# Taking a kernel's short first load from its large group instead of from one contiguous megabyte, with three stores in place of four

## The chip, the cores and the metric

The kernel runs on one core of one Trainium2 chip. The metric is the time of one execution on the device, in microseconds (us). The trace records every DMA packet.

## The reference

```python
batch, channels, length = 32, 256, 4096          # x: 134 MB of fp32
output_size = 256
for i in range(output_size):
    start = int(i * length / output_size)
    end = int((i + 1) * length / output_size)
    result[:, :, i] = np.max(x[:, :, start:end], axis=-1)
```

Each output is the maximum of 16 neighbouring inputs. Nothing is reused: 134.22 MB are read and 8.39 MB are written.

## The kernel before

One window is 16 floats, 64 bytes. There are 16,384 windows for each of 128 partitions. They are fetched in 20 loads, all issued by SyncE, into three slots of one large tile. VectorE reduces each load, and the results collect at the top of the same tile. Loads are at first 1,024 windows (64 KB) per partition and shrink as the results take room. The first load is short, 128 windows (8 KB), so that VectorE has something to do early.

```python
    slot_sizes = [MOST]                              # MOST = 1024 windows
    rounds = [[FIRST] + [MOST] * (SLOTS - 1)]        # FIRST = 128, SLOTS = 3
    # ... later rounds shrink: 1000, 940, 884, 832, 784, 736+152 ...
    sizes = [n for r in rounds for n in r]
    groups = [sizes[:1], sizes[1 : ROUNDS_A * SLOTS], sizes[ROUNDS_A * SLOTS :]]
    # ...
    for g, loads in enumerate(groups):
        n = sum(loads)
        xg = xw[first : first + P * n].rearrange("(p n) w -> p (n w)", p=P)
        og = ow[first : first + P * n].rearrange("(p n) -> p n", p=P)
        # ...
        for i, size in enumerate(loads):
            a = b - size
            # ...
            nc.sync.dma_start(out=slot, in_=xg[:, a * W : b * W])
            nc.vector.reduce_max(out=area[:, base + a : base + b], in_=..., axis=X)
        # ...
        if g < len(groups) - 1:
            stores.append((og, area[:, base : base + n]))
        else:                                        # LAST = 4: the last four loads apart
            end = sum(loads[len(loads) - LAST :])
            for a, b in ((end, n), (0, end)):
                stores.append((og[:, a:b], area[:, base + a : base + b]))
    for dst, src in stores[1:2] + stores[0:1] + stores[2:]:
        nc.sync.dma_start(out=dst, in_=src)
```

A group is a contiguous part of x that is dealt out to the partitions. So a group of n windows per partition has a distance of 64 n bytes between the rows of two neighbouring partitions: its partition pitch. The first group is 128 windows: one contiguous megabyte, in 128 rows of 8 KB. The second is 7,868 windows (pitch 491.75 KB, KB being 1,024 bytes), the third 8,388 windows (524.25 KB).

## Time and profile before

| | before |
|---|---|
| time, median of 3 | 335.2 us (335.18 to 335.23) |
| moved over the span | 142.61 MB, 428 GB/s |
| DMA queue busy | 99.2% of the span |
| VectorE busy | 83% |

From the page of the kernel before: the span, VectorE's busy time and share, DMA packets, the DMA queue's share of 16 engines' span, and the costliest group of instructions with VectorE's idle time and what ended it.

```profile
span 333.4 us, 113 instructions
DVE 276.0 (83%) x20; POOL 0.2 (0%) x4
DMA packets 3456, 142.61 MB, mean 428 GB/s; under 512 B 384, under 2 KB 512, under 8 KB 512
q1 hardware_dynamic: 3456, 142.61, 99.2%
L82 DVE TENSOR_REDUCE area<-area 128x1000 f32<-128x16000 f32 (+8 forms) x20 | 276.0, 13806 | 49.2 <-DMA area<-in_x_dram 49.2
```

The queue's 99.2% is what counts. VectorE is busy 83% and waits for loads in the rest; the DMA engines hardly wait for anything. The Trainium skill, "DMA: Bandwidth & Descriptors", section "Bandwidth", gives 425 GB/s as measured for one large load into all partitions (16 MB, issued there from GpSimd, here from SyncE), and 435 as the ceiling. The trace agrees: the second and third load, 8.39 MB each, end 19.35 us apart, which is 434 GB/s.

The start in the timeline of the kernel before (start, duration, engine and instruction, then the idle time ahead of it and what ended it):

```profile
5.60 2.29 DVE L82 TENSOR_REDUCE area<-area 128x128 f32<-128x2048 f32 x1 [5.60 <-DMA area<-in_x_dram]
24.95 17.22 DVE L82 TENSOR_REDUCE area<-area 128x1024 f32<-128x16384 f32 x1 [17.06 <-DMA area<-in_x_dram]
44.30 17.22 DVE L82 TENSOR_REDUCE area<-area 128x1024 f32<-128x16384 f32 x1 [2.13 <-DMA area<-in_x_dram]
63.20 16.82 DVE L82 TENSOR_REDUCE area<-area 128x1000 f32<-128x16000 f32 x1 [1.68 <-DMA area<-in_x_dram]
```

The stores among its DMA issues (transfer, engine and operation, count, KB of one, us from issue to landing):

```profile
out_dram<-area SPq DMA_DIRECT2D x1, 3934.0 KB, 27.4
out_dram<-area SPq DMA_DIRECT2D x1, 2966.0 KB, 33.7
out_dram<-area SPq DMA_DIRECT2D x1, 1228.0 KB, 7.3
out_dram<-area SPq DMA_DIRECT2D x1, 64.0 KB, 27.1
```

Their 27 and 34 us are queueing: the first three are issued at about 295 us, behind loads that last until 312 us. The last waits for the last reduce and is issued at 325.2 us, while the engines are still busy until 329 us with the store before it. So nothing at the end is exposed except the 1.3 us between the last completion write (332.07 us) and the end of the span.

### The profile page before, as it was taken

The page shows a single profiled execution, that of the slowest core. Times are in us where ns is not written, and L with a number is a line of the kernel's source. Part 1 is how long each engine was busy: PE and PEld are TensorE (multiplying, and loading weights), DVE is VectorE, ACT ScalarE, POOL GpSimd, SP SyncE. Part 2 cuts the span into 40 slices and gives each one's busy share as a digit, 9 for nine tenths or more (in the row PEclk, how much of TensorE's full clock was granted, in tenths as well). Part 3 has the DMA queues.
Part 4 walks back from the last instruction along what each step waited for, and adds up shares of the span by engine and source line. Part 5 has one row for each costly group of instructions (what it writes and reads, how often), then busy time and mean ns, then how long its engine had stood idle before and what let it go on. Part 6 is the DMA issues. An engine that isn't in the chain of part 4 may idle for free.

```text
span 333.4 us, 113 instructions
## 1 busy us (share of the span) xinstructions
DVE 276.0 (83%) x20; POOL 0.2 (0%) x4
## 2 busy tenths in 40 slices
DVE  2009979797988989797989797989898898989990
POOL 0000000000000000000000000000000000000000
DMA  9898989898989998999999999999999999999997
GB/s 377 377 503 377 503 369 491 369 491 369 491 369 462 462 462 346 462 462 441 434 434 434 434 434 415 409 409 505 415 409 433 433 433 433 433 416 452 391 432 333
DMA packets 3456, 142.61 MB, mean 428 GB/s; under 512 B 384, under 2 KB 512, under 8 KB 512
## 3 DMA queue, kind: packets, MB, share of 16 engines
q1 hardware_dynamic: 3456, 142.61, 99.2%
HBM read 134.22 MB, written 8.39 MB: 428 GB/s over the span
## 4 chain that ended last, share of the span: by engine, by line
DMA 64%; DVE 31%; DVEq 1%; another core or an unknown queue 0%; SPq 0%; issue 0%
DMA area<-in_x_dram 64%; DVE area L82 31%; DVEq L129 1%; SPq L81 0%; DVEq L82 0%
## 5 line engine op out<-in xcount | busy, mean ns | idle before, releaser
L82 DVE TENSOR_REDUCE area<-area 128x1000 f32<-128x16000 f32 (+8 forms) x20 | 276.0, 13806 | 49.2 <-DMA area<-in_x_dram 49.2
L115 POOL MEMSET const-bfloat16-1.0<- 128x1 bf16 x1 | 0.1, 102 | 0.0
L115 POOL MEMSET const-uint8-127<- 128x1 uint8 x1 | 0.1, 102 | 0.0
L115 POOL MEMSET const-float32-0.0<- 128x1 f32 x1 | 0.1, 99 | 0.2 <-issue 0.2
L115 POOL MEMSET const-float32-1.0<- 128x1 f32 x1 | 0.1, 99 | 0.0
## 6 DMA issues: line engine op xcount, KB each, us to landing
area<-in_x_dram SPq DMA_DIRECT2D x3, 8000.0 KB, 39.9
area<-in_x_dram SPq DMA_DIRECT2D x3, 7520.0 KB, 37.5
area<-in_x_dram SPq DMA_DIRECT2D x3, 7072.0 KB, 35.3
area<-in_x_dram SPq DMA_DIRECT2D x3, 6656.0 KB, 33.2
area<-in_x_dram SPq DMA_DIRECT2D x3, 6272.0 KB, 31.3
area<-in_x_dram SPq DMA_DIRECT2D x1, 5888.0 KB, 30.3
out_dram<-area SPq DMA_DIRECT2D x1, 3934.0 KB, 27.4
out_dram<-area SPq DMA_DIRECT2D x1, 2966.0 KB, 33.7
```

Of the source, the lines that this page charges most:

```text
L82: nc.vector.reduce_max(out=area[:, base + a : base + b], in_=slot.rearrange("p (n w) -> p n w", w=W), axis=mybir.AxisListType.X,)
L115: nc = _bacc.Bacc("TRN2", target_bir_lowering=False, num_devices=1)
L129: with _tile.TileContext(nc) as tc:
```

## The change

The intent: one group fewer, so one store fewer. The store that falls away is the short one, with rows of 512 bytes. In exchange the first load's rows come from the large group, which grows to 7,996 windows (pitch 499.75 KB); they no longer form one contiguous megabyte.

```diff
-    groups = [sizes[:1], sizes[1 : ROUNDS_A * SLOTS], sizes[ROUNDS_A * SLOTS :]]
+    groups = [sizes[: ROUNDS_A * SLOTS], sizes[ROUNDS_A * SLOTS :]]
...
-    for dst, src in stores[1:2] + stores[0:1] + stores[2:]:
+    for dst, src in stores:
         nc.sync.dma_start(out=dst, in_=src)
```

Sizes and order of the loads, VectorE's instructions and the addresses in the tile stay the same.

## The prediction

> **What bounds the kernel now.** The page gives 428 GB/s and a DMA queue 99.2% busy; VectorE is busy 276.0 of 333.4 us, and its 49.2 us of idle time are waits for loads. The packet records show data moving without a gap from 1.75 us to the last completion write at 332.07 us: loads until about 312.4, the 31,472-byte rows of the large store until 321.8, the 512-byte rows of the small store (0.195 us of each engine), the 23,728-byte rows until 329.1, the last 9,824-byte rows. So the span is the sum of the transfers on each of 16 engines, with 1.75 us before and 1.3 us after. Only transfer time, start-up latency or a new hole changes it. The last store is issued at 325.2 us, 3.4 us before its engines come free.
>
> **What the change does, costed.**
> 1. It removes the small store: eight 512-byte packets per engine (24 ns apart) and a completion write of under 10 ns, 0.20 us of each engine. The bytes return as 512 more in each of eight 31 KB rows, at 26.9 GB/s: 8 x 19 ns = 0.15 us. Net gain 0.05 us.
> 2. The first large group's pitch becomes 499.75 KB instead of 491.75. The Trainium skill, "DMA: Bandwidth & Descriptors", "Latency and other measured facts", reports [...]full rate at a padded large pitch. This trace has the mirror case: the second group's pitch is 524.25 KB, 12.25 KB above 512 where the new one is 12.25 below; the two sum to 1 MB. Its rows run at 27.0 GB/s per engine, spread under 1% (50,176 bytes in 1.853 to 1.864 us), like the first group's. I expect no aliasing and no change for loads 2 to 9.
> 3. The first load reads 8 KB rows 499.75 KB apart instead of one contiguous megabyte. Now: first packets take 0.3 to 1.3 us (median near 0.95), all later ones 0.309, which is full rate; VectorE starts at 5.60 us. The second load already begins at scattered rows directly behind 8 KB packets, and its first 64 KB packets take 2.418 us, full rate too: a scattered row's first access is hidden behind one 8 KB packet. So only the very first packets can be longer, by 0 to 0.5 us, my estimate from their present spread. All of it is critical: nothing later has a hole to absorb it.
> 4. VectorE's instructions, SBUF addresses and the order of loads stay; the first slot is released near 7.9 us, some 35 us before its next load is needed.
>
> **Sum.** -0.05 us (store) + 0.15 us (start) = +0.1: 335.3 us, range 334.9 to 336.3. Chances: faster by over 2% 1%, within 2% 97%, slower by over 2% 2%.
>
> **What would show it.** Right: first reduce at 5.5 to 6.2 us; later reduces shifted by the same amount; later 8 KB packets at 0.309 us; 64,000-byte rows at 2.36 us; no 512-byte packets; last store's rows directly after the second's. Wrong at 2 if packets of loads 2 to 9 take longer; wrong at 3 if later 8 KB packets exceed 0.309 us or the landing moves by over 0.7 us.
>
> **What would make it wrong.** Address conflicts at the new pitch (tens of us if they halve the rate of half the loads); a start-up stall on every scattered 8 KB packet (8 x 0.5 = 4 us at most).

## The result

| | before | changed |
|---|---|---|
| median of 6 runs, same chip | 335.19 us (335.16 to 335.23) | 335.09 us (334.88 to 335.18) |
| ratio | | 0.9996, 95% interval 0.9983 to 1.0009 |

Ratios are the mean time of one kernel's fast runs over that of the other's in the same rounds, so not quite the ratio of the medians.

The changed kernel's page:

```profile
span 333.4 us, 112 instructions
DVE 276.0 (83%) x20; POOL 0.2 (0%) x4
DMA packets 3312, 142.61 MB, mean 428 GB/s; under 512 B 368, under 2 KB 368, under 8 KB 368
q1 hardware_dynamic: 3312, 142.61, 99.1%
L81 DVE TENSOR_REDUCE area<-area 128x1000 f32<-128x16000 f32 (+8 forms) x20 | 276.0, 13806 | 49.1 <-DMA area<-in_x_dram 49.1
```

There are 144 packets fewer: 128 rows of 512 bytes and 16 completion writes. There is one instruction fewer, and no busy time, rate or share on the page moves by more than 0.1. Its timeline at the start:

```profile
5.22 2.29 DVE L81 TENSOR_REDUCE area<-area 128x128 f32<-128x2048 f32 x1 [5.22 <-DMA area<-in_x_dram]
24.71 17.22 DVE L81 TENSOR_REDUCE area<-area 128x1024 f32<-128x16384 f32 x1 [17.20 <-DMA area<-in_x_dram]
44.26 17.22 DVE L81 TENSOR_REDUCE area<-area 128x1024 f32<-128x16384 f32 x1 [2.33 <-DMA area<-in_x_dram]
63.17 16.82 DVE L81 TENSOR_REDUCE area<-area 128x1000 f32<-128x16000 f32 x1 [1.69 <-DMA area<-in_x_dram]
```

And its stores among the DMA issues:

```profile
out_dram<-area SPq DMA_DIRECT2D x1, 3998.0 KB, 27.6
out_dram<-area SPq DMA_DIRECT2D x1, 2966.0 KB, 34.2
out_dram<-area SPq DMA_DIRECT2D x1, 1228.0 KB, 7.4
```

One line is odd. The first reduce begins 0.38 us earlier with the scattered rows, where the prediction had it 0.15 us later. By the third reduce only 0.04 us of that is left. The packet records show where it went: the first load's packets cost less, but some rows of loads 2 and 3 took up to 2.56 us instead of 2.42. The engines' ends, worked out from the completion writes of each load (mean of 16 engines, and the last one):

```
                     load 1           load 3            last load          end of all stores
before   mean/last   4.973 / 5.174    43.644 / 43.833   312.280 / 312.487  331.841 / 332.063
changed  mean/last   4.737 / 4.872    43.481 / 43.926   312.116 / 312.514  331.652 / 332.040
```

The mean engine keeps 0.16 us of the early start to the last load, but the last engine keeps none, and the kernel ends with the last one. Is the early start the change's doing, or did this one execution happen to have it? That is the first question for the experiments.

### The profile page after: what moved, and what is told of

It is laid out like the page before. It is cut to its first block, busy times and chain, and to the rows that moved or that the text cites. A ratio compares the mean times of both kernels' runs of the same rounds, so it can differ in the third digit from the quotient of the medians.

```text
span 333.4 us, 112 instructions
## 1 busy us (share of the span) xinstructions
DVE 276.0 (83%) x20; POOL 0.2 (0%) x4
## 3 DMA queue, kind: packets, MB, share of 16 engines
HBM read 134.22 MB, written 8.39 MB: 428 GB/s over the span
## 4 chain that ended last, share of the span: by engine, by line
DMA 64%; DVE 31%; DVEq 1%; another core or an unknown queue 0%; SPq 0%; issue 0%
DMA area<-in_x_dram 64%; DVE area L81 31%; DVEq L128 1%; SPq L80 0%; DVEq L81 0%
```

## The experiments

(A completion write is the 4-byte packet with which each engine ends each transfer; "the mean engine" is the mean of the 16 engines' times.) Theory A: the contiguous megabyte costs the start some tenths of a microsecond, and scattering its rows wins them. Rival B: the start varies from run to run, and only the store's price is the change's own. Each session below is a set of kernels run on one chip with the kernel before among them. Session 1 is the result above; session 2 ran on chip 9, session 3 (the later sections) on chip 4, sessions 4 and 5 on chip 12. Because the tail is far more regular than the start, the stores are compared by the time of the mean engine from its last load's completion to its final completion.

### Both kernels again, and each part of the change alone

The kernel before and the changed one, unaltered:

> The kernel before, once more, for a second profile. If the slow start is a property of the contiguous first megabyte, first 8 KB packets again take about 0.95 us in the median, the start costs about 0.7 us per engine over full rate, and the first reduce starts at 5.6 us. If the start differs by chance from run to run, these numbers will differ by 0.2 us or more from the first profile. Time 335.2 us.

> The changed kernel, once more. Theory (scattered first rows start faster): first reduce at about 5.2 us, start costs about 0.35 us per engine, one or two engines lose 0.2 to 0.4 us in loads 2 to 4 again. Rival (chance): these numbers wander, and the first reduce may be at 5.6 us or later. Time 335.1 us, ratio to before 0.9997.

The loads of the change with the small store put back:

```diff
-            stores.append((og, area[:, base : base + n]))
+            cut = n - FIRST
+            for a, b in ((0, cut), (cut, n)):
+                stores.append((og[:, a:b], area[:, base + a : base + b]))
```

> The changed kernel with its large store cut in two, so that the 512-byte rows and the fourth store are back while the loads stay scattered. If the store is worth 0.05 us: the mean engine's end moves back by 0.05 us (0.20 us for the small store against 0.15 us), time about 335.15 us. If the store were what made the change faster, the time returns to 335.2 us and the start stays at 5.2 us.

The stores of the change with the contiguous first load put back (the first 128 windows are wrong):

```diff
-            nc.sync.dma_start(out=slot, in_=xg[:, a * W : b * W])
+            src = xg[:, a * W : b * W]
+            if n_loads == 0:
+                src = xw[: P * size].rearrange("(p n) w -> p (n w)", p=P)
+            nc.sync.dma_start(out=slot, in_=src)
```

> The changed kernel with only the first load taken from the contiguous first megabyte of x (results of the first 128 windows wrong on purpose); pitch of the large group and the three stores as in the change. If contiguity costs the start: first reduce at 5.6 us, 0.7 us per engine, time about 335.15 us (only the store's 0.05 us is left). If chance: start as in the changed kernel, 5.2 us.

In later sessions, three more looks at the start. First, the changed kernel a third time:

> The changed kernel a third time, in a session of its own. If the 0.1 us of the first session (335.09 against 335.19 us) and its early start (first reduce at 5.22 us) were chance: 335.18 us, first reduce near 5.55 us, third load's mean landing near 43.62 us. If scattered rows can gain 0.1 us: a time of 335.1 us or less, and a third load's landing near 43.5 us.

Second, the kernel before with only its first load scattered:

```diff
-            nc.sync.dma_start(out=slot, in_=xg[:, a * W : b * W])
+            src = xg[:, a * W : b * W]
+            if n_loads == 0:
+                src = xw[P * size : P * (size + 7868)].rearrange("(p n) w -> p (n w)", p=P)[:, (7868 - size) * W : 7868 * W]
+            nc.sync.dma_start(out=slot, in_=src)
```

> The kernel before with only the first load's source changed: 8 KB rows 491.75 KB apart, from the large group (first 128 windows wrong on purpose); the small store stays. If scattering costs or saves the start anything, first reduce and third load's landing move against 5.5 to 5.6 and 43.61 to 43.65 us, as by the prediction's 0.15 us later; if not, they stay and the time is 335.2 us.

Third, the contiguous variant of the changed kernel once more:

> The changed kernel with the contiguous first load once more, in another session (first 128 windows wrong on purpose). So far the first reduce began at 5.53 to 5.60 us in three profiles with a contiguous first load, and at 5.22, 5.28, 5.54, 5.54, 5.58 and 5.63 us in six with a scattered one. If the early start is chance, it may show here too, at 5.2 to 5.3 us; if only scattered rows can have it, this is again 5.5 to 5.6 us. One look can show that a contiguous load has early starts, and cannot show that it has none. Last load to end, mean engine: 22.476 us again.

(The 22.476 us in this text counts from the end of the last load but one; the table below counts from the last load.) What was measured, with the two first profiles:

| session | run | first load | small store | first reduce, us | load 3, mean engine | last load to end, mean engine | time, median | the kernel before in that session |
|---|---|---|---|---|---|---|---|---|
| 1 | before | contiguous | yes | 5.60 | 43.644 | 19.562 | 335.19 | |
| 1 | changed | scattered | no | 5.22 | 43.481 | 19.536 | 335.09 | 335.19 |
| 2 | before_again | contiguous | yes | 5.53 | 43.607 | 19.563 | 335.16 | 335.19 |
| 2 | after_again | scattered | no | 5.54 | 43.607 | 19.540 | 335.18 | 335.19 |
| 2 | after_split_store | scattered | yes | 5.54 | 43.647 | 19.632 | 335.20 | 335.19 |
| 2 | after_first_contiguous | contiguous | no | 5.57 | 43.652 | 19.540 | 335.22 | 335.19 |
| 4 | after_third | scattered | no | 5.28 | 43.475 | 19.540 | 335.11 | 335.38 |
| 4 | before_first_scattered | scattered, 491.75 KB | yes | 5.63 | 43.563 | 19.562 | 335.21 | 335.38 |
| 5 | after_first_contiguous_2 | contiguous | no | 5.64 | 43.699 | 19.540 | 335.23 | 335.24 |

The first reduce in four of these looks: before_again, after_again, after_third and after_first_contiguous_2.

```profile
5.53 2.29 DVE L82 TENSOR_REDUCE area<-area 128x128 f32<-128x2048 f32 x1 [5.53 <-DMA area<-in_x_dram]
5.54 2.29 DVE L81 TENSOR_REDUCE area<-area 128x128 f32<-128x2048 f32 x1 [5.54 <-DMA area<-in_x_dram]
5.28 2.29 DVE L81 TENSOR_REDUCE area<-area 128x128 f32<-128x2048 f32 x1 [5.28 <-DMA area<-in_x_dram]
5.64 2.29 DVE L84 TENSOR_REDUCE area<-area 128x128 f32<-128x2048 f32 x1 [5.64 <-DMA area<-in_x_dram]
```

*The start.* The same changed kernel began its first reduce at 5.54 us in session 2, so the 0.38 us of the first profile is not something that scattered rows always win. Nor do they cost the predicted 0.15 us: 5.54 us lies within the contiguous looks, 5.53 to 5.64. Theory A in its plain form falls. The packets say so too: the time that an engine's eight 8 KB packets took over eight times 0.309 us was 0.69 us in the first profile of the kernel before, but 0.40 us in before_again, where 0.7 was expected, and lies at 0.27 to 0.69 us in the four contiguous looks and at 0.35 to 0.65 us in the six scattered ones. What remains is that early starts (5.22 and 5.28) came in two of five looks at the changed kernel's loads (after_8_small_stores, below, has 5.58), and in none of four with a contiguous first load. In after_third the expectation for a real gain was met (335.11 us, load 3 at 43.475 us). But the kernel before was slow in that session (335.38 us), and the other scattered start there, before_first_scattered, had 5.63 us and 335.21 us. With so few looks, chance is not ruled out, nor a difference between chips, and neither is an early start that only scattered rows can have. Even where it came, it did not reach the end in the profile: in after_third the mean engine's load 3 ended at 43.475 us, but its last load at 312.305, later than in the first profile of before (312.280), because rows of loads 2 to 12 ran slow here and there (60,160-byte rows took up to 2.453 us instead of 2.22). Slow rows are no mark of scattered first rows or of an early start: after_first_contiguous_2 had 64 KB rows of up to 2.634 us, with neither, in the slowest execution of its set (335.70 us). The two executions with an early start were also the slowest of their sets (335.18 and 335.45 us), so it stays open whether the faster ones, which have no trace, kept the early start.

*The stores.* Here the columns hardly scatter. In the kernel before, again, and with a scattered first load 19.562, 19.563 and 19.562 us pass; with the change's stores 19.536 and four times 19.540, whichever way the first load is read. So the change's store part is worth 0.02 us of the mean engine, not 0.05. To split this by store, each engine's packets have to be followed in the records, each beginning where the engine's last one ended. Sorting the completion writes by time does not do: the engines are some 0.4 us apart and the small store lasts only 0.2 us, so the writes of two stores mix. Engine by engine:

```
mean engine, us           large store (with the small one)   second store   last store
before                    9.335 + 0.195 = 9.530              7.060          2.972
before_again              9.336 + 0.195 = 9.531              7.061          2.972
changed                   9.482                              7.075          2.979
after_again               9.484                              7.077          2.979
after_split_store         9.334 + 0.194 = 9.528              7.126          2.977
```

The small store takes 0.195 us and its bytes in long rows 0.149 us (9.484 less 9.335), a difference of 0.046 us, as predicted. But the second store, which has the same rows in both kernels, is 0.017 us longer in the changed one (its 23,728-byte rows take 0.8871 and 0.8874 us in the mean instead of 0.8852), and the last 0.007 us longer. The first load has no part in it: after_first_contiguous has 9.484, 7.077 and 2.978. Why the same rows are slower was not found. Putting the small store back behind the longer pitch cost 0.09 us of the mean engine (19.632 against 19.540), not the expected 0.05: half of that is the small store again, and half is the second store, whose first rows took 0.940 us there, 0.892 in the changed kernel and 0.882 in the kernel before. So a small store ahead does not by itself make the rows behind it slower.

### Multiplying the price of a small store

The difference above is too small to see in a time, so the suspected cost was multiplied.

```diff
-            stores.append((og, area[:, base : base + n]))
+            cuts = [0] + [n - k * FIRST for k in range(8, -1, -1)]
+            for a, b in zip(cuts, cuts[1:]):
+                stores.append((og[:, a:b], area[:, base + a : base + b]))
```

> The changed kernel with its large store cut into one of 6,972 windows per partition and eight of 128 (512-byte rows). The prediction's price (0.20 us for a small store against 0.15 us for the same bytes in long rows) makes the mean engine's end 8 x 0.05 = 0.4 us later, all of it in the span: about 335.6 us. The price that the four profiles so far show, from the end of the last load to the end of the large store's bytes (9.551 against 9.483 us), makes it 8 x 0.07 = 0.55 us. If the end of the kernel hides it, 335.2 us.

Measured: 336.12 us (336.05 to 336.57) against 335.18 for the kernel before, ratio 1.003, interval 1.0017 to 1.0042. The price is in the span, as expected, but it is larger than either sum. The page and its DMA issues:

```profile
DMA packets 4464, 142.61 MB, mean 427 GB/s; under 512 B 496, under 2 KB 1520, under 8 KB 1520
out_dram<-area SPq DMA_DIRECT2D x1, 3486.0 KB, 26.4
out_dram<-area SPq DMA_DIRECT2D x1, 2966.0 KB, 8.7
out_dram<-area SPq DMA_DIRECT2D x8, 64.0 KB, 25.8
```

The mean engine needs 20.57 us from its last load to the end, 1.03 more than the changed kernel. By the row records 8.281 us of this are the large store, 7.106 the second and 2.988 the last (7.077 and 2.979 in the changed kernel), which leaves 2.196 us for the eight small stores: 0.275 us each, where a single one took 0.195. The bytes of one piece take 0.150 us in long rows ((9.484 - 8.281) / 8), so each piece costs 0.12 us and all eight 0.99; only 0.04 us lies in the stores behind them. The 512-byte packets themselves became longer along the row of small stores, from 0.027 us among the first 256 to 0.036 us later on; the mean is 0.033. Why was not found. The prediction, which priced one small store, came to less than half. (The 0.07 us in the expectation came from completion writes sorted by time, the mixing described above; followed engine by engine it is 0.05.)

### The pitch

The prediction quoted from the Trainium skill a halved rate at a row pitch of 512 KiB. That is a misreading. The page ("DMA: Bandwidth & Descriptors", section "Latency and other measured facts") has 207 GB/s at 512 KiB, beside 214 for full rate; the halved figure, 103, belongs to 4 and 8 MiB, and 2 MiB has 164, all for copies between HBM tensors. So four runs asked what an exact power of two does in this kernel. "The page" in their expectations is this one, and the times worked out there from its figures are estimates.

One group, a pitch of exactly 1 MB, two stores, results right:

```diff
-    groups = [sizes[: ROUNDS_A * SLOTS], sizes[ROUNDS_A * SLOTS :]]
+    groups = [sizes]
```

> The changed kernel with one group, so that every load has a partition pitch of exactly 1 MB; two stores; results right. If a pitch at a power of two aliases, by the halving that the prediction wrongly attributed to 512 KB, 65,536-byte rows would take about 5 us and the time is near 640 us; between the figures that the page really has for 512 KB (207 of 214 GB/s) and 2 MB (164), rows take 3 to 30% longer: 345 to 420 us. If the pitch does not matter here: rows at 2.42 us and 335.2 us.

The same with the loads' pitch 8 KB shorter (source rows overlap, results wrong):

```diff
-            nc.sync.dma_start(out=slot, in_=xg[:, a * W : b * W])
+            src = bass.AP(tensor=x.tensor, offset=a * W, ap=[[(n - 128) * W, P], [1, size * W]])
+            nc.sync.dma_start(out=slot, in_=src)
```

> The one-group kernel with the partition pitch made 8 KB less than 1 MB in the loads and nothing else changed (overlapping source rows, results wrong on purpose). If the 8.7 us of the one-group kernel were the exact power of two, rows return to 2.42 us and the time to 335.2 us, as the page says of 4 KB of padding. If they came of having one group, or of any pitch near a power of two, the time stays near 344 us.

Both groups at exactly 512 KB, by a longer first load, and a control with the same loads and other pitches:

```diff
-    FIRST = 128
+    FIRST = 348
-    ROUNDS_A = 3        # (control only)
+    ROUNDS_A = 4
```

> The changed kernel with a first load of 348 windows instead of 128, which makes both groups 8,192 windows: a pitch of exactly 512 KB in every load. By the page's figure at 512 KB (207 of 214 GB/s, 3%): rows of 64 KB at 2.5 us and a time near 345 us; if the pitch does not matter: 2.42 us, 335 to 336 us.

> Control of pitch_512: the same loads and instructions of VectorE, the groups cut one round later, so that the pitches are 677 and 347 KB. Rows at full rate, 2.42 us; 335 to 336 us. The difference of the two is the pitch's alone, but for the stores' row lengths.

| pitch of the loads | time, median | range | the kernel before in that session |
|---|---|---|---|
| 1 MB | 343.88 us | 342.77 to 345.80 | 335.18 |
| 1 MB less 8 KB | 335.21 us | 335.12 to 335.50 | 335.38 |
| 512 KB, both groups | 335.82 us | 335.57 to 336.81 | 335.18 |
| 677 and 347 KB (control) | 335.28 us | 335.27 to 335.35 | 335.18 |

An exact 1 MB costs 8.7 us (ratio 1.0248, interval 1.0226 to 1.0270), and 8 KB less restores it all, in one group and with two stores. An exact 512 KB costs about 0.5 us against its control: the 64 KB rows take 2.427 us instead of 2.420 in the mean, the 63,744-byte rows 2.372 instead of 2.354. That is under 1% in these rows, less than the 3% between the page's two figures. The two kernels' store rows differ in length as well.

The unexpected part is when the 1 MB kernel pays. Its timeline (loads 2 to 8; the traced execution was the slowest of its set, 345.80 us):

```profile
28.78 17.22 DVE L81 TENSOR_REDUCE area<-area 128x1024 f32<-128x16384 f32 x1 [20.53 <-DMA area<-in_x_dram]
50.27 17.22 DVE L81 TENSOR_REDUCE area<-area 128x1024 f32<-128x16384 f32 x1 [4.27 <-DMA area<-in_x_dram]
71.34 16.82 DVE L81 TENSOR_REDUCE area<-area 128x1000 f32<-128x16000 f32 x1 [3.85 <-DMA area<-in_x_dram]
90.69 16.82 DVE L81 TENSOR_REDUCE area<-area 128x1000 f32<-128x16000 f32 x1 [2.53 <-DMA area<-in_x_dram]
109.72 16.82 DVE L81 TENSOR_REDUCE area<-area 128x1000 f32<-128x16000 f32 x1 [2.21 <-DMA area<-in_x_dram]
129.06 15.82 DVE L81 TENSOR_REDUCE area<-area 128x940 f32<-128x15040 f32 x1 [2.52 <-DMA area<-in_x_dram]
146.79 15.82 DVE L81 TENSOR_REDUCE area<-area 128x940 f32<-128x15040 f32 x1 [1.92 <-DMA area<-in_x_dram]
```

The eighth load's reduce in the kernel before:

```profile
136.55 15.82 DVE L82 TENSOR_REDUCE area<-area 128x940 f32<-128x15040 f32 x1 [1.89 <-DMA area<-in_x_dram]
```

What moved in four stretches of that kernel (from and to, length, VectorE and GpSimd busy with counts, TensorE's clock, mean DMA share, GB/s):

```profile
6.00:44.00 38.00, 17.47 (x2) 0.00 (x0) 1.00 0.99 381
44.00:63.00 19.00, 14.73 (x2) 0.00 (x0) 1.00 1.00 389
63.00:82.00 19.00, 15.14 (x2) 0.00 (x0) 1.00 0.97 408
82.00:101.00 19.00, 16.47 (x2) 0.00 (x0) 1.00 1.02 441
```

And in the same stretches of the kernel with 8 KB less:

```profile
6.00:44.00 38.00, 19.19 (x2) 0.00 (x0) 1.00 1.01 439
44.00:63.00 19.00, 17.22 (x1) 0.00 (x0) 1.00 1.01 435
63.00:82.00 19.00, 16.82 (x1) 0.00 (x0) 1.00 1.00 431
82.00:101.00 19.00, 16.82 (x1) 0.00 (x0) 1.00 0.99 428
```

The rate is 381 GB/s at first and rises; VectorE's idle time ahead of the eighth load's reduce, 1.92 us, is again that of the kernel before (1.89), and the mean engine takes 17.74 us for load 9, against 17.75 in the changed kernel. From there the loads but the very last run at full rate. Meanwhile the engines drift apart: their completions of one load spread over 0.6 us at load 1, 2.3 at load 3 and 3.9 at load 9, where the same kernel with 8 KB less stays under 0.9 us throughout. That fits engines that collide while they walk their rows in step and stop colliding once they are out of step; no run tests that reading. The spread is paid once more at the end: the last engine finishes 2.4 us after the mean one.

None of these kernels beats the changed one. Apart from stray slow rows, its engines move data at full rate without a gap from 1.74 us to 332.0 us, and no run here shortened that by more than the scatter of the times.

## Why the prediction was right or wrong

The time lies in the range. That is less than it sounds: the range also holds the time of the kernel before, and the forecast sum of +0.1 us appeared in no session. Every term was small. Point by point:

- *The bound.* Right. The queue is 99% busy in both, and added store work went straight into the span (after_8_small_stores, 0.94 us).
- *Step 1, the store, -0.05 us.* Right for the small store itself: 0.195 us of each engine against 0.15 us for the same bytes in long rows. The sum lacked that the two later stores become 0.024 us longer, so that -0.02 us is left. Nor does the price multiply: eight small stores in a row cost 1.03 us instead of 0.4, because each took 0.275 us.
- *Step 2, the pitch, no change.* Right: apart from stray slow rows, rows of loads 2 to 9 take the same time (64,000 bytes in 2.364 us before, 2.365 after). The reference was misquoted: 512 KB is not a pitch of half rate, and here it costs 0.5 us. The argument that carried was the trace's own: the third group runs at full rate at the mirror pitch.
- *Step 3, the start, +0.15 us.* This is the step that failed. At pitches of 491.75 and 499.75 KB no scattered start (5.63 us at the latest) came after the latest contiguous one (5.64); twice it came some 0.3 us earlier. (At other pitches, 1 MB less 8 KB began at 5.69 us and exactly 1 MB at 5.96, one look each.) The range of "0 to 0.5 us longer" was taken from one trace and allowed only one direction. The part that said later 8 KB packets would run at 0.309 us held for nearly all of them: 8 of 112 took longer in the first profile of the changed kernel, up to 0.599 us, but 2 did in that of the kernel before, up to 0.861.
- *"Nothing later has a hole to absorb it."* No run delayed the start by much. Small differences did reach the end in the mean engine: from before to before_again its load 1 ends 0.032 us earlier and its last store too. An early start was not kept. In the two profiles that had one, slow rows in some engines used it up, and the kernel ends with the last engine.
- *The sum.* Predicted +0.1, measured -0.10 in session 1, -0.01 in session 2, -0.27 in session 4 (where the kernel before was 0.14 to 0.20 us slower than in the other sessions). Each session's interval for the ratio includes 1. Only 0.02 us of it is explained; whether the rest is chance or an early start in runs without a trace stays open.

## What to carry to other kernels

When the DMA queue is busy without a gap, rearranging which rows a load takes is worth what it changes in packet time, and that is found by comparing completion times per engine rather than spans. A difference seen at the start of one profile is not an effect until a second profile of the same kernel shows it. Keep partition pitches off exact powers of two (at 1 MB, 8 KB less was enough). Do not multiply the price of one short store: eight in a row took 0.275 us each where one took 0.195. And when a time is split by completion writes, follow each engine; a transfer shorter than the distance between the engines is misread when the writes are only sorted by time.

## What the Trainium skill lacked or had wrong

- "DMA: Bandwidth & Descriptors", "Latency and other measured facts", has the loss at large power-of-two pitches for copies between HBM tensors only, and as independent of how many tiles are touched. For loads into SBUF at exactly 1 MB the loss was not constant: the 8.39 MB of load 2 took the mean engine 22.55 us instead of 19.33, and full rate was back by load 9, when the engines had drifted 3.9 us apart. At 512 KB it was under 1% in the long rows, 0.5 us in all.
- The same row gives 4 KB of padding as enough at 4 MB and has no figure for 1 MB. Here a pitch 8 KB short of 1 MB brought the full rate back (335.21 us instead of 343.88); no run tried 4 KB.
- The same page, "Specifications", gives 512 bytes as the least transfer for line rate. Here 512-byte store rows followed one another at 24 ns per engine, 21 GB/s, where rows of 31 KB ran at 26.9; among eight such stores a packet took 0.033 us in the mean.
- No page has what stores of short rows cost on this chip when several follow one another: eight took 0.275 us of each engine apiece, a single one 0.195.
- No page says how much the start of a kernel's first load varies: the first reduce of one and the same kernel began at 5.22, 5.54 and 5.28 us in three sessions.
